# A two-branch encoder layer on one core: first loads in order of need, combinations in six pieces, the first mixer low parts on GpSimd, denominators in one operation, zero halves kept

## The chip, the cores and the metric

The kernel runs on one core of one Trainium2 chip, in one launch. The metric is the device time of an execution in microseconds (us). The engines are PE (TensorE, the matrix engine), ACT (ScalarE), DVE (VectorE), POOL (GpSimd) and SP (SyncE, which here only issues DMAs). All but SP compute; each works through its own list of instructions in the listed order and waits on semaphores for the others.

## The reference

One encoder layer is applied with shared weights to two inputs, `x_prompt` (1024 tokens, called A in the kernel) and `x_sample` (512 tokens, called B), model width 1024, everything in float32.

```python
def encoder_layer(x, ...):
    h = rms_norm(x, pre_w)
    cols = jnp.einsum('bsd,dc->bsc', h, w_in)
    m_qk, m_v, m_o, m_z, m_i, m_f, a_qkv, a_z, gate = jnp.split(cols, ...)
    y_m = mlstm_mixer(m_qk, m_v, m_o, m_i, m_f, ...) * jax.nn.silu(m_z)
    y_a = dilated_attention(a_qkv, rel_table) * jax.nn.silu(a_z)
    p_m = jnp.einsum('bsc,cd->bsd', y_m, w_pm)
    p_a = jnp.einsum('bsc,cd->bsd', y_a, w_pa)
    g = jax.nn.sigmoid(gate).reshape(b_, s_, N_BRANCHES, D_MODEL)
    merged = g[:, :, 0] * p_m + g[:, :, 1] * p_a
    out = jnp.einsum('bsd,de->bse', merged, w_out)
    return x + rms_norm(out, post_w)

def mlstm_scan(q, k, v, li, lf):          # per direction, 4 heads of 256, chunks of 128 tokens
    def step(carry, xs):
        ...
        num = jnp.einsum('nhts,nhsv->nhtv', sc, vc) + wa[..., None] * jnp.einsum('nhtk,nhkv->nhtv', qc, c_mat)
        den = jnp.sum(sc, axis=-1) + wa * jnp.einsum('nhtk,nhk->nht', qc, n_vec)
        h = num / jnp.maximum(jnp.abs(den), jnp.exp(-mt))[..., None]
        ...
```

The mLSTM runs forward and backward, and each head's sum of both is normalized. The attention has three groups of 8 heads of 64 with windows and dilations (128, 1), (512, 4), (2048, 16); each group adds a bias by relative distance (`rel_table`).

## The kernel before

**Arithmetic.** Every float32 product is made of three matmuls: each operand is split into a high part (rounded by a copy on ACT, `fp32r`) and a low part (the difference, made on DVE or POOL). `mm3` (L192 to L194) issues high × high, high × low, low × high into one PSUM bank. So ahead of any product stand an ACT copy and a subtraction.

**Stages.** The span begins with the values and gates of B (`short_values`, to about 145 us), then come the projections of A (to 1074), then four stages in which PE fills its waits with projections of B and of the mixers: the mLSTM of A (1095 to 1382), the attention of A, the mLSTM of B (`mlstm_short`), the attention of B with the closing projections.

**The start.** `short_values` (L356) works through eight blocks of 322 weight columns, `vw` tiles `va` and `vb` in turn, each in two halves `kh` (128x1288). A half is split into `vhi` (ACT, L375) and `vlo` (DVE, L376) and multiplied by the high and low parts `Hh`, `Hl` of B's transposed input, 96 matmuls of 128x322 a block in four banks `d`, one for each 128 tokens. The results are scaled by the inverse root of each token's mean square and copied out to `vz` (ACT L398, DVE L399) or `avz`. The loop loads block b+2 at its end, since its tile is then free.

Beside it run the roots: `scale(i)` (L1768) loads the rows of B, or one of two halves of A, ACT sums the squares (L255, one operation of 128x1024 for each 128 tokens), POOL makes the inverse root `xr` (L256, L257). `spread(i)` (L1774) turns four such columns into a row that is the same on all partitions: DVE puts each on a diagonal `dg` (L1777), PE multiplies them by ones, ACT copies the result to `R` (L313). With `R`, `combos` (L325) makes from A's transposed input `xq` the operands of A's projections, which are done with seven products of block matrices instead of eight: norms (L317), sums and differences, and their high and low parts (L321, L322).

**The order of the work.** From the start to 1074 us the order on each engine is set by a scheduler of the compiler, by priorities and by the order in the code; `tc.high_priority()` puts the block splits ahead, and `tc.issue_after(x)` keeps what is in its block behind instruction x on that engine's list. From the mixers on, the order of PE and SP is the order of the code. There loads go through a list: `queue` adds one, `tick` (once a round) issues `pace` of them, and `need` issues all up to the one asked for.

**The transition.** The last projections of A are two gates each (`gates(j, c)`); the first mixer unit of B is a dense projection with weights `wraw`, split into `wh` (ACT, L248) and `wl` (DVE, L249), on B's input `xs`, split by `short_input` (L640) into `H`.

**The mLSTM rounds.** A round is (head, chunk, direction), 64 in all for A. `front(k+1)` prepares the next round's operands, `core(k)` multiplies. Value tiles (`V0a` to `V1b`) have 258 columns: 256 values, a column of ones, which sums the denominator in the same product `num`, and a column of zeros. DVE makes the denominator in two operations and inverts it; in the second half of the chunks ACT squares and scales the sum `X` to `hn`, and three rounds later PE transposes it (L984):

```python
r = sb.tile([P, 4], F32, name="r", bufs=4)
nc.vector.tensor_scalar(r[:, 0:1], pn[:, 256:257], m["fl"], None, op0=OP.max)
nc.vector.scalar_tensor_tensor(r[:, 1:2], pn[:, 256:257], -1.0, r[:, 0:1], op0=OP.mult, op1=OP.max)
nc.vector.reciprocal(r[:, 2:3], r[:, 1:2])
```

**The attention units.** A unit u (0 to 11) is a pair of heads of one group. Units of the dilated groups whose sequence is 128 long are called narrow (8 of 12 for B, 4 of 12 for A). `att_load` puts a narrow unit's keys into `V0a`, `V0b`, `V1a`, `V1b` in such a way that each head's half is zero in the other head's place, with memsets on POOL (L1275), and queues the loads; `table` loads a unit's bias table as the unit begins.

Of the kernel before, what the change touches and what calls it, by code (L numbers as in the profile page):

```python
# [29 lines left out]
P = 128  # L30
# [145 lines left out]
class Net:  # L176
    def __init__(self, tc, a):
        self.tc, self.nc, self.a = tc, tc.nc, a
        self.clock = self.lag = 0
        self.pending, self.owner = [], {}  # L180
        self.defer, self.mixed, self.rows = False, set(), {}
        self.queued, self.pace = [], 1

# [59 lines left out]
    def split_w(self, raw, n):  # L243
# [3 lines left out]
        self.wsplit.append((hi, lo))  # L247
        self.splits = (nc.scalar.activation(hi[:, :n], raw[:, :n], AF.Copy),  # L248
                       nc.vector.tensor_sub(lo[:, :n], raw[:, :n], hi[:, :n].bitcast(F32)))  # L249
# [69 lines left out]
    def parts(self, hl, k, x):  # L319
        hi, lo = hl[0][:, k], hl[1][:, k]  # L320
        end = self.nc.scalar.activation(hi, x[:, k], AF.Copy)  # L321
        self.nc.vector.tensor_sub(lo, x[:, k], hi.bitcast(F32))  # L322
        return end

    def combos(self, H, xq, R):  # L325
# [12 lines left out]
        for k in range(4):  # L338
            self.norm(a1, 0, k, R[1])
            self.norm(b1, 1, k, R[1])  # L340
        for k in range(4):
# [16 lines left out]
    def short_values(self, T, H, load, vw, sb, ps, r, first, places):  # L358
# [5 lines left out]
        for b in range(8):  # L364
            raw = raws[b % 2]
            banks = [ps.tile([P, BLK], F32, name="d") for _ in range(4)]
            for kh in range(2):
                hi, lo = places.pop(0) if places else (vw.tile([P, N], F32R, name=x, bufs=2) for x in ("vhi", "vlo"))
                with self.tc.high_priority():
                    parts = 4 if b == 0 else 1  # L370
                    for i in range(parts):
# [4 lines left out]
                        nc.vector.tensor_sub(lo[:, c], raw[:, kh, c], hi[:, c].bitcast(F32))  # L376
                if b == 0:
                    load(kh, 4)
                wh, wl = (z.rearrange("p (k c) -> p k c", c=VW) for z in (hi, lo))
# [6 lines left out]
            if b < 6:  # L386
                raws[b % 2] = vw.tile([P, 2, N], F32, name=("va", "vb")[b % 2], bufs=1)
                fetch(b + 2)
            c0 = VW * b
            for t in range(4):  # L390
# [4 lines left out]
                if a0 < a1:  # L395
                    z, x = sb.tile([P, 2, VW], F32R, name="vz", bufs=3), p[:, a0 - c0:a1 - c0]
# [5 lines left out]
                if a0 < c0 + VW:  # L402
                    z, w = sb.tile([P, VW], F32, name="avz", bufs=3), c0 + VW - a0
# [236 lines left out]
    def short_input(self, xt):  # L640

        for q in range(2):
            for k in range(4):
                end = self.parts(self.hT[q], k, xt[q])
# [167 lines left out]
    def ml_load(self, T, h):  # L812
# [12 lines left out]
        for i, x in enumerate([both[0][:, :1032], both[0][:, 1032:]] if S == BLK else both):  # L825
            x = x.rearrange("p (n c) -> p n c", c=258)
            nc.gpsimd.memset(x[:, :, 256:257].bitcast(F32), 1.0 - i)
            nc.gpsimd.memset(x[:, :, 257:258].bitcast(F32), 0.0)
# [6 lines left out]
    def mlstm(self, T, fill, steps, first, banks, lead, after, beside=()):  # L835
# [10 lines left out]
        with ExitStack() as stack:  # L846
# [13 lines left out]
            fill.stage(steps, lead + len(rounds) + n // 4 + 3)  # L860
# [66 lines left out]
            def core(k):  # L927
# [37 lines left out]
                nc.vector.tensor_scalar(r[:, 0:1], pn[:, 256:257], m["fl"], None, op0=OP.max)  # L965
                nc.vector.scalar_tensor_tensor(r[:, 1:2], pn[:, 256:257], -1.0, r[:, 0:1], op0=OP.mult, op1=OP.max)
# [37 lines left out]
            for k, (h, i, d) in enumerate(rounds):  # L1004
# [16 lines left out]
                turns.pop(k - 3, lambda: None)()  # L1021
# [1033 lines left out]
```

## Time and profile before

| | us |
|---|---|
| median of 3 executions | 2307.6 (2307.18 to 2310.66) |
| the profiled execution | 2305.97 |
| its span, first to last instruction | 2304.2 |
| PE busy in the span | 2240.8 (97%) |
| DVE, ACT, POOL busy | 1483.5, 1104.3, 619.0 |

The mean granted clock of TensorE is 0.992. "Busy" counts an engine's instructions, register and DMA-issuing ones left out. A row of the timeline gives start, length, engine, line, operation, `output<-inputs`, shape and count, and in brackets the idle time of the engine just before it with what ended that. A row of the waits says for whom an engine waited, in all, how often, and the longest.

### The profile page before, as it was taken

The page shows a single profiled execution, that of the slowest core. Times are in us where ns is not written, and L with a number is a line of the kernel's source. Part 1 is how long each engine was busy: PE and PEld are TensorE (multiplying, and loading weights), DVE is VectorE, ACT ScalarE, POOL GpSimd, SP SyncE. Part 2 cuts the span into 40 slices and gives each one's busy share as a digit, 9 for nine tenths or more (in the row PEclk, how much of TensorE's full clock was granted, in tenths as well). Part 3 has the DMA queues.
Part 4 walks back from the last instruction along what each step waited for, and adds up shares of the span by engine and source line. Part 5 has one row for each costly group of instructions (what it writes and reads, how often), then busy time and mean ns, then how long its engine had stood idle before and what let it go on. Part 6 is the DMA issues. An engine that isn't in the chain of part 4 may idle for free. (4 is left out here: it accounts for less than half of the span.)

```text
span 2304.2 us, 35360 instructions
## 1 busy us (share of the span) xinstructions
PE 2240.8 (97%) x12210; PEld 1955.1 (85%) x12210; DVE 1483.5 (64%) x2890; ACT 1104.3 (48%) x2255; POOL 619.0 (27%) x824
## 2 busy tenths in 40 slices
PE   8999999999999999998999999999999999999998
PEld 7999998888887888887888889989888888878787
DVE  3857656767888765644788876675477744555563
ACT  5534223434444433333777766676644444544332
POOL 1000003333333222230567650001033221421321
PEclk8999999999999999999999999999999999999999
DMA  9446424555422222434766569988777787686673
GB/s 360 146 122 155 130 95 171 195 192 194 153 107 104 92 83 93 149 111 143 260 213 208 153 175 241 239 232 213 205 240 253 236 255 229 190 261 195 214 258 113
DMA packets 253627, 425.05 MB, mean 184 GB/s; under 512 B 26208, under 2 KB 150752, under 8 KB 252680
## 3 DMA queue, kind: packets, MB, share of 16 engines
q1 hardware_dynamic: 249848, 410.20, 57.4%
q10 hardware_dynamic: 3600, 12.59, 1.4%
q8 instruction: 97, 1.59, 0.3%
q14 instruction: 82, 0.67, 0.1%
HBM read 302.72 MB, written 128.37 MB: 187 GB/s over the span
## 5 line engine op out<-in xcount | busy, mean ns | idle before, releaser
L192 PE MATMUL dense<-H,wh 128*128 128x512 f32 x672 | 281.1, 418 | 3.8 <-ACT wh L248 3.8
L194 PE MATMUL dense<-H,wl 128*128 128x512 f32 x672 | 265.6, 395 | 1.9 <-DVE wl L249 1.9
L193 PE MATMUL dense<-H,wh 128*128 128x512 f32 x672 | 264.8, 394 | 0.0
L194 PE MATMUL d<-Hh,phla 128*128 128x512 f32 x608 | 236.9, 390 | 1.8 <-DVE phla L527 1.8
L193 PE MATMUL d<-Hl,phla 128*128 128x512 f32 x608 | 236.6, 389 | 0.0
L192 PE MATMUL d<-Hh,phla 128*128 128x512 f32 x608 | 236.5, 389 | 0.0
L192 PE MATMUL d<-vhi,Hh 128*128 128x322 f32 x704 | 222.6, 316 | 7.4 <-ACT vhi L375 7.4
L193 PE MATMUL d<-vlo,Hh 128*128 128x322 f32 x704 | 222.3, 316 | 6.1 <-DVE vlo L376 6.1
L194 PE MATMUL d<-vhi,Hl 128*128 128x322 f32 x704 | 222.1, 316 | 0.0
L249 DVE TENSOR_TENSOR wl<-wraw,wh 128x1024 fp32r<-128x1024 f32 x110 | 138.3, 1258 | 80.1 <-ACT wh L248 74.5
L1371 DVE CUSTOM_DVE_ANT_0 ls<-lg,bias 128x256 f32<-128x256 f32 (+1 forms) x288 | 93.7, 362 | 148.5 <-PE lg L1359 60.9
L545 POOL TENSOR_TENSOR psum_w<-pw_raw 128x512 f32<-128x512 f32 x38 | 56.6, 1489 | 465.3 <-DMA pw_raw<-w_in 424.9
L192 PE MATMUL d<-Hh,phlb 128*128 128x512 f32 x456 | 177.4, 389 | 0.0
L193 PE MATMUL d<-Hl,phlb 128*128 128x512 f32 x456 | 177.4, 389 | 0.0
L194 PE MATMUL d<-Hh,phlb 128*128 128x512 f32 x456 | 177.4, 389 | 0.0
L1375 ACT ACTIVATE ls<-ls,nm 128x256 f32<-128x256 f32 (+1 forms) x288 | 130.0, 453 | 93.4 <-DVE nm L1373 83.4
L194 PEld LDWEIGHTS dense<-H,wl 128*128 128x128 f32 x672 | 126.9, 189 | 31.7 <-DVE wl L249 2.6
L248 ACT ACTIVATE wh<-wraw 128x1024 fp32r<-128x1024 f32 x110 | 115.7, 1053 | 72.4 <-PE dense L193 33.4
L192 PEld LDWEIGHTS d<-vhi,Hh 128*128 128x128 f32 x704 | 135.3, 192 | 9.2 <-ACT vhi L375 8.1
L192 PEld LDWEIGHTS dense<-H,wh 128*128 128x128 f32 x672 | 127.5, 190 | 17.5 <-ACT wh L248 4.2
L193 PEld LDWEIGHTS d<-vlo,Hh 128*128 128x128 f32 x704 | 135.2, 192 | 7.4 <-DVE vlo L376 7.4
L193 PEld LDWEIGHTS dense<-H,wh 128*128 128x128 f32 x672 | 127.7, 190 | 13.4
(558 smaller groups left out, 5708.3 us busy)
## 6 DMA issues: line engine op xcount, KB each, us to landing
pw_raw<-w_in SPq DMA_DIRECT2D x76, 512.0 KB
wraw<-w_in SPq DMA_DIRECT2D x76, 512.0 KB
aqk_a<-pwk SPq DMA_DIRECT2D x48, 512.0 KB
aqk_b<-sw SPq DMA_DIRECT2D x48, 256.0 KB
wraw<-w_pm SPq DMA_DIRECT2D x24, 512.0 KB
wraw<-w_out SPq DMA_DIRECT2D x24, 512.0 KB
vb<-w_vp SPq DMA_DIRECT2D x16, 644.0 KB
va<-w_vp SPq DMA_DIRECT2D x14, 644.0 KB
```

The source lines that it names most:

```text
L192: nc.tensor.matmul(out, lh, rh, start=start, stop=False)
L193: nc.tensor.matmul(out, lh, rl, start=False, stop=False)
L194: nc.tensor.matmul(out, ll, rh, start=False, stop=stop)
L248: self.splits = (nc.scalar.activation(hi[:, :n], raw[:, :n], AF.Copy), nc.vector.tensor_sub(lo[:, :n], raw[:, :n], hi[:, :n].bitcast(F32)))
L249: nc.vector.tensor_sub(lo[:, :n], raw[:, :n], hi[:, :n].bitcast(F32)))
L545: self.nc.gpsimd.tensor_add(s[:, 0], ws[1][:, 0], ws[1][:, 1])
L1371: nc.vector.tensor_tensor_reduce(out=ls[:, hh], in0=ts["lg"][hh], in1=bt[:, hh], scale=1.0, scalar=NEG, op0=OP.add, op1=OP.max, accum_out= ...
L1375: nc.scalar.activation(ls[:, hh], ls[:, hh], AF.Exp, bias=nm[:, hh:hh + 1], accum_out=ot[:, 128 + hh:129 + hh])
```

## The change

It has eight parts.

1. The first loads are issued in another order (below), and the loads of block b+2 ahead of block b's matmuls, in `short_values`. `spread(1)` comes after block 1 and `spread(2)` after block 2, instead of both after block 2. Pools: `vz` 3 to 8 buffers, `avz` 3 to 2, `dg` 8 to 4.
2. `combos` is cut into six pieces instead of five, and each stands behind the low part of a block's second split (`N.low`) on its engine.
3. The first mixer unit's weight low part `wl` and the low parts of the first half of B's input go from DVE to POOL (`low_on`, `on`), and `short_input` stands behind the two weight splits.
4. The column of zeros of the value tiles becomes −1, so that `num` holds the denominator with both signs, and one operation takes the largest of three.
5. `hn` is transposed four rounds later instead of three, for A.
6. A narrow unit's key tile with its zero halves is kept for the next one but one (`narrow`), so only the first two do the memsets.
7. A narrow unit also queues the bias table of the next unit (`tables`).
8. Line numbers move by 2 to 26.

```diff
-    def parts(self, hl, k, x):
+    def parts(self, hl, k, x, on=None):
         hi, lo = hl[0][:, k], hl[1][:, k]
         end = self.nc.scalar.activation(hi, x[:, k], AF.Copy)
-        self.nc.vector.tensor_sub(lo, x[:, k], hi.bitcast(F32))
+        (on or self.nc.vector).tensor_sub(lo, x[:, k], hi.bitcast(F32))
...
         for k in range(4):
             self.norm(a1, 0, k, R[1])
             self.norm(b1, 1, k, R[1])
+        yield
         for k in range(4):
             sub(a0[:, k], a1[:, k], a0[:, k])
...
-                        nc.vector.tensor_sub(lo[:, c], raw[:, kh, c], hi[:, c].bitcast(F32))
-                if b == 0:
-                    load(kh, 4)
-                wh, wl = (z.rearrange("p (k c) -> p k c", c=VW) for z in (hi, lo))
+                        self.low = nc.vector.tensor_sub(lo[:, c], raw[:, kh, c], hi[:, c].bitcast(F32))
+                split.append([z.rearrange("p (k c) -> p k c", c=VW) for z in (hi, lo)])
+            if b == 0:
+                load(1, 4)
+            if b < 6:
+                raws[b % 2] = vw.tile([P, 2, N], F32, name=("va", "vb")[b % 2], bufs=1)
+                fetch(b + 2)
+            if b == 0:
+                load(1, 5)
+            for kh, (wh, wl) in enumerate(split):
                 for i in range(4):
...
-            if b < 6:
-                raws[b % 2] = vw.tile([P, 2, N], F32, name=("va", "vb")[b % 2], bufs=1)
-                fetch(b + 2)
...
-                end = self.parts(self.hT[q], k, xt[q])
+                end = self.parts(self.hT[q], k, xt[q], None if q else self.nc.gpsimd)
...
-            nc.gpsimd.memset(x[:, :, 256:257].bitcast(F32), 1.0 - i)
-            nc.gpsimd.memset(x[:, :, 257:258].bitcast(F32), 0.0)
+            if i:
+                nc.gpsimd.memset(x[:, :, 256:258].bitcast(F32), 0.0)
+            else:
+                for c in range(2):
+                    nc.gpsimd.memset(x[:, :, 256 + c:257 + c].bitcast(F32), 1.0 - 2 * c)
...
-            fill.stage(steps, lead + len(rounds) + n // 4 + 3)
+            fill.stage(steps, lead + len(rounds) + n // 4 + 4)
...
-                nc.vector.tensor_scalar(r[:, 0:1], pn[:, 256:257], m["fl"], None, op0=OP.max)
-                nc.vector.scalar_tensor_tensor(r[:, 1:2], pn[:, 256:257], -1.0, r[:, 0:1], op0=OP.mult, op1=OP.max)
+                nc.vector.tensor_scalar(r[:, 1:2], pn[:, 256:257], m["fl"], pn[:, 257:258], op0=OP.max, op1=OP.max)
...
-                turns.pop(k - 3, lambda: None)()
+                turns.pop(k - 4, lambda: None)()
...
+        kept = None if wide else self.narrow.get((S, u % 2))
...
+                    if kept is None:
+                        nc.gpsimd.memset(k[i][rows, :, 1 - side].bitcast(F32), 0.0)
...
             b0 = table(0)
+            if u < 11:
+                self.tables[u + 1] = bias()[:, :2 * P].rearrange("p (h w) -> p h w", h=2)
+                self.table_load(T, u + 1, 0, self.tables[u + 1])
...
-                    elif j:
-                        scale(0)
+                    elif k == 4:
                         for kh in range(2):
                             weights(1, kh)
-                        xq.extend([xp.tile([P, 4, BLK], F32, name=f"xq{2 * i + j}") for j in range(2)] for i in range(2))
-                        for i in range(2):
-                            scale(1 + i)
-                        for i in range(2):
-                            for j in range(2):
-                                nc.sync.dma_start(xq[i][j], a[x1 + "_t"][i, j])
+                        scale(0)
+                    else:
+                        scale(1)
+                        inputs(0)
+                        scale(2)
...
                 next(steps)
+                spread(1)
+                inputs(1)
                 next(steps)
-                for i in (1, 2):
-                    spread(i)
+                spread(2)
...
-                for b, _ in enumerate(steps):
+                with tc.issue_after(N.low.ins):
                     next(combos)
+                for b, _ in enumerate(steps):
+                    with tc.issue_after(N.low.ins):
+                        next(combos)
...
+            N.low_on.append(nc.gpsimd)
...
-            end = N.short_input(xt)
+            with tc.issue_after(N.splits[0].ins), tc.issue_after(N.splits[1].ins):
+                end = N.short_input(xt)
```

The order on SP at the start, before. `vb` and `va` of shape 128x1288 are the weight halves of blocks 1, 2 and 3, `Hh_…` and `Hl_…` loaded from `x_sample` and `x_prompt` are rows for the roots (they lie in buffers of later operands), and `xq` is A's transposed input.

```order
L1771 DMA Hh_102<-x_sample 128x1024 x2
L1771 DMA Hl_109<-x_sample 128x1024 x2
L1763 DMA vb<-w_vp 128x1288 x2
L1771 DMA Hh_101<-x_prompt 128x1024 x2
L1771 DMA Hl_108<-x_prompt 128x1024 x2
L1771 DMA Hh_99<-x_prompt 128x1024 x2
L1771 DMA Hl_106<-x_prompt 128x1024 x2
L1805 DMA xq_283<-x_prompt_t 128x2048
L1805 DMA xq_284<-x_prompt_t 128x2048
L1805 DMA xq_285<-x_prompt_t 128x2048
L1805 DMA xq_286<-x_prompt_t 128x2048
L362 DMA va<-w_vp 128x1288 x2
```

The same place after it:

```order
L1779 DMA vb<-w_vp 128x1288 x2
L1787 DMA Hh_102<-x_sample 128x1024 x2
L1787 DMA Hl_109<-x_sample 128x1024 x2
L1787 DMA Hh_101<-x_prompt 128x1024 x2
L1787 DMA Hl_108<-x_prompt 128x1024
L365 DMA va<-w_vp 128x1288 x2
L1787 DMA Hl_108<-x_prompt 128x1024
L1824 DMA xq_254<-x_prompt_t 128x2048
L1824 DMA xq_255<-x_prompt_t 128x2048
L1787 DMA Hh_99<-x_prompt 128x1024 x2
L1787 DMA Hl_106<-x_prompt 128x1024 x2
```

Block 1's weights moved ahead of all rows, block 2's ahead of one row tile of A's first half and all of the second; two `xq` loads and then the weights of block 3 follow behind these rows.

The order on ACT around blocks 2 and 3, before (`R_144`, `R_145` are the rows that `spread(1)` and `spread(2)` make, `xr` the columns of roots):

```order
L375 ACTIVATE vhi<-vb 128x1288
L398 ACTIVATE vz<-d,xr_131 128x322
L398 ACTIVATE vz<-d,xr_132 128x322
L398 ACTIVATE vz<-d,xr_133 128x322
L375 ACTIVATE vhi<-vb 128x1288
L398 ACTIVATE vz<-d,xr_134 128x322
L313 ACTIVATE R_144<-d 128x512
L313 ACTIVATE R_145<-d 128x512
L321 ACTIVATE Hh_98<-xq_283 128x512 x4
```

After it, from block 1's third copy to the first half of the combinations:

```order
L405 ACTIVATE vz<-d,xr_133 128x322
L257 ACTIVATE Hl_108,xr_138<-Hl_108 128x1024
L379 ACTIVATE vhi<-va 128x1288
L405 ACTIVATE vz<-d,xr_134 128x322
L315 ACTIVATE R_144<-d 128x512
L323 ACTIVATE Hh_98<-xq_254 128x512 x4
```

And a few rows on, at block 3's split:

```order
L257 ACTIVATE Hl_106,xr_142<-Hl_106 128x1024
L276 ACTIVATE cws<-cws 128x32
L277 ACTIVATE cws<-cws 128x32
L315 ACTIVATE R_145<-d 128x512
L379 ACTIVATE vhi<-vb 128x1288 x2
L405 ACTIVATE vz<-d,xr_131 128x322
```

A root of A's first half now stands among block 1's copies, with `R_144` right behind them, and `R_145` has moved ahead of both high parts of block 3.

The order on POOL at the transition, before (`V0a` to `V1b` are the value tiles, `sraw` a buffer of the mixers):

```order
L563 TENSOR_TENSOR psum_w<-pw_raw,psum_w 128x512 x2
L827 MEMSET V0a 128x8
L828 MEMSET V0a 128x8
L827 MEMSET V0b 128x8
L828 MEMSET V0b 128x8
L827 MEMSET V1a 128x8
L828 MEMSET V1a 128x8
L827 MEMSET V1b 128x8
L828 MEMSET V1b 128x8
L590 MEMSET sraw 128x1
```

After it:

```order
L570 TENSOR_TENSOR psum_w<-pw_raw,psum_w 128x512 x2
L838 MEMSET V0a 128x8 x2
L835 MEMSET V0b 128x8x2
L838 MEMSET V1a 128x8 x2
L835 MEMSET V1b 128x8x2
L251 TENSOR_TENSOR wl_8709<-wraw_8706,wh_8708 128x1024
L324 TENSOR_TENSOR H_8721<-xs_7664,H_8720 128x512 x4
L597 MEMSET sraw 128x1
```

The weight's low part and four low parts of the input came from DVE; they stand behind the memsets of the value tiles. On DVE remain the low parts of the second weight and of the second input half.

40 lines of the change are left out of this document (24 added, 16 removed).

## The prediction

> **What bounds the kernel now.** I read the page's first part, then busy time in stretches of the span (each row: from and to, length, busy us and instructions of PE, its weight loads, DVE, ACT and POOL, then the granted clock, the DMA share and GB/s), then what TensorE (PE) waits for (us in total, times, longest), and last the timeline at each place that the diff touches.
>
> ```profile
> PE 2240.8 (97%) x12210; PEld 1955.1 (85%) x12210; DVE 1483.5 (64%) x2890; ACT 1104.3 (48%) x2255; POOL 619.0 (27%) x824
> 145.00:691.00 546.00, 546.00 (x2860) 485.10 (x2860) 391.28 (x480) 206.92 (x243) 130.40 (x104) 1.00 0.46 152
> 1095.00:1382.00 287.00, 275.26 (x1724) 244.79 (x1724) 229.22 (x552) 208.16 (x517) 178.03 (x313) 0.99 0.64 202
> 20.00:90.00 70.00, 56.70 (x340) 55.21 (x339) 40.14 (x65) 35.77 (x64) 7.61 (x19) 0.88 0.76 267
> 90.00:130.00 40.00, 40.00 (x272) 40.00 (x271) 21.37 (x29) 17.87 (x28) 0.34 (x2) 1.00 0.44 150
> 48.00:58.00 10.00, 10.00 (x61) 10.00 (x61) 2.71 (x4) 2.25 (x6) 0.00 (x0) 0.88 1.02 322
> 1165.90:1176.00 10.10, 10.10 (x52) 8.96 (x53) 6.83 (x19) 7.42 (x21) 6.29 (x18) 0.83 0.48 145
> 2072.40:2082.00 9.60, 9.54 (x37) 7.83 (x38) 4.66 (x18) 5.12 (x17) 2.03 (x3) 0.71 1.01 279
> PE d L192 <- ACT vhi L375: 7.4, 2, 4.3
> PE d L193 <- DVE vlo L376: 6.1, 4, 4.1
> PE a L984 <- ACT hn L977: 6.3, 4, 2.2
> PE num L192 <- ACT X L969: 2.0, 3, 1.1
> PE num L192 <- DVE r L966: 1.8, 1, 1.8
> PE a L1183 <- ACT hn L1176: 5.5, 6, 1.3
> ```
>
> PE is busy for 2240.8 of 2304.2 us, so 63.4 us of idle time, and whatever a lowered clock costs, is all that a reordering can win. From 145 to 691 us PE has no idle time at all: what the start gains shifts the rest forward whole. The waits name where much of the 63.4 lies: value splits 13.5, mLSTM transposes 6.3, their counterpart of the short batch 5.5.
>
> The start loses more than its gaps. From 90 to 130 us, at full clock and without a gap, 272 matmuls pass in 40 us, 6.80 a microsecond. The 340 of the stretch from 20 to 90 would need 50.0 us and took 70: 20.0 us lost. Busy time of 56.70 leaves 13.3 us of gaps; the other 6.7 is the granted clock, 0.88 on average there, and low even in a row without a gap (48 to 58: 61 matmuls in 10 us instead of 68).
>
> **Part 1: first loads and block splits.** The three gaps and what they stand on:
>
> ```profile
> 23.45 0.64 PE L192 MATMUL d<-vhi,Hh 128*128 128x322 f32 x1 [3.11 <-ACT vhi L375]
> ...
> 46.01 0.64 PE L192 MATMUL d<-vhi,Hh 128*128 128x322 f32 x1 [4.32 <-ACT vhi L375]
> ...
> 83.75 0.42 PE L193 MATMUL d<-vlo,Hh 128*128 128x322 f32 x1 [4.08 <-DVE vlo L376]
> 44.68 1.28 ACT L375 ACTIVATE vhi<-va 128x1288 fp32r<-128x1288 f32 x1 [10.48 <-DMA va<-w_vp]
> 68.05 10.02 DVE L317 SCALAR_TENSOR_TENSOR xq<-xq,prew,R 128x512 f32<-128x512 f32 x15
> 77.98 4.30 DVE L322 TENSOR_TENSOR Hl<-xq,Hh 128x512 fp32r<-128x512 f32 x7
> 82.20 1.50 DVE L376 TENSOR_TENSOR vlo<-va,vhi 128x1288 fp32r<-128x1288 f32 x1
> ```
>
> Block 1 (gap at 23.45) splits its weights on ACT behind row sums whose rows were loaded first. Block 2's weights arrive at 44.68, last of the line. The new order puts 6.5 MB behind them (four 1 MB `xq` pieces, five 512 KB row tiles), 20 to 24 us at the 322 and 267 GB/s of the rows above, so they come between 20 and 25; block 1, which could start at 20.3 (23.45 − 3.11), ends near 35. At 82.20 the low part stands behind 14 us of combinations, queued on DVE without regard to it; in six pieces behind the splits it goes ahead of them. These gaps, their second halves and the clock behind them go: up to 20.0 us.
>
> Two waits come instead, both read from the order. First, PE now does `spread(1)` right after block 1, and its fourth diagonal needs a row sum that ACT makes among the value copies of block 1. Second, in block 3 ACT writes `R_145` (from `spread(2)`, after block 2 on PE) ahead of both high parts `vhi<-vb`. Prices:
>
> ```profile
> 26.68 1.06 ACT L255 ACTIVATE Hl<-Hl 128x1024 f32<-128x1024 f32 x1
> 30.75 0.55 POOL L257 TENSOR_TENSOR xr<-xr,mhalf 128x1 f32<-128x1 f32 x1
> 65.40 0.86 DVE L1777 TENSOR_SCALAR dg<-ident,xr 128x128 f32<-128x128 f32 x4
> 66.86 1.08 ACT L313 ACTIVATE R<-d 128x512 f32<-128x512 f32 x2
> ```
>
> Row sum 1.06, its POOL root 0.55, a diagonal 0.22: 1.8 us, of which the copies of block 1 hide little; with the steps between engines I take 2 us of idle PE. Block 3: R 0.54, high part 1.28, then the low part, 1.50: 3.3 us. Together 5.3. The gap of 1.85 us shown further down is followed by a granted clock of 0.83 over 10.10 us (the row from 1165.90), 1.7 us lost; with one such loss the new waits cost 7.0, and the start gives 20.0 − 7.0 = 13. Ends: both waits hidden, 20; each half as long again and two clock losses, 11.3, so 8.7. The combinations cost nothing while DVE has room: a block is 96 matmuls at 6.80, 14.1 us, a piece of 12 operations at 0.67 (10.02 by 15) 8.0, two low parts 3.0. If that cover is gone, PE waits for what a piece overruns. **−13.**
>
> **Part 2: low parts of the first mixer projection on GpSimd.**
>
> ```profile
> 1077.70 0.66 PE L192 MATMUL dense<-H,wh 128*128 128x512 f32 x1 [3.77 <-ACT wh L248]
> ...
> 1080.66 0.79 PE L194 MATMUL dense<-H,wl 128*128 128x512 f32 x1 [1.88 <-DVE wl L249]
> 1074.58 4.90 DVE L322 TENSOR_TENSOR H<-xs,H 128x512 fp32r<-128x512 f32 x8
> 1079.39 2.35 DVE L249 TENSOR_TENSOR wl<-wraw,wh 128x1024 fp32r<-128x1024 f32 x2
> 1074.00 0.11 POOL L827 MEMSET V0a<- 128x8 f32 x1 [20.64 <-PE d L194]
> 522.12 4.90 DVE L631 SCALAR_TENSOR_TENSOR pwk<-c,pwk 128x1024 fp32r<-128x1024 f32 x2 [1.69 <-ACT pwk L630]
> 522.94 2.32 POOL L545 TENSOR_TENSOR psum_w<-pw_raw 128x512 f32<-128x512 f32 x1 [5.56 <-DMA pw_raw<-w_in]
> L563 POOL TENSOR_TENSOR psum_w<-pw_raw,psum_w x38: 1287/1302/1742, 347.2 to 1052.1; 128x512 f32<-128x512 f32 x38
> ```
>
> Here PE waits 3.77 for ACT's high parts, then 1.88 for DVE, which makes eight 128x512 low parts (0.61 each) before the weight's. Now ACT has the high parts done before PE's last pair ends (the order puts them ahead of the last copies of `gates(7)`), so the first wait goes. But `wl` and four low parts stand on POOL behind the memset that waits for PE until 1074.00: at 1.30 for 128x512, 2.6 + 4 × 1.30 = 7.8 us, to about 1082.1; the second matmul runs at about 1078.2, and one k-step per 1.30 after it. Before, the fourth k-step ended at about 1084.5: three steps of three matmuls, 0.43 each at the low clock there, after 1080.66. So −2.4. The other end is contention: POOL took 2.32 instead of 1.30 beside DVE's two-input operation at 522, and DVE owes 1.2 + 4 × 0.61 = 3.7 us of its own; if all of that excludes POOL, the fourth step is at 1085.8, +1.3. Neither row is nearer, so I take **−1**. [...]
>
> **Part 3: mLSTM rounds.** Dropping one of two denominator operations shortens DVE by 64 × 0.156, 10 us, and some 5 in the short batch; PE gains only where it waits for `r`. Transposes one round later (`k-4`) let PE find `hn` ready:
>
> ```profile
> 1165.90 0.36 PE L192 MATMUL num<-V0a,sch 128*128 128x258 f32 x1 [1.85 <-DVE r L966]
> L966 DVE SCALAR_TENSOR_TENSOR r<-num,r x64: 139/156/161, 1103.2 to 1364.9; 128x1 f32<-128x1 f32 x64
> ```
>
> A round is 287/64 = 4.5 us, longer than the longest wait on `hn` (2.2), so all 6.3 can go. Late next is `num`: 2.0 us on `X`, 1.85 on `r`, with DVE busy 80% (229.22 of 287). I let 1.3 come back: **−5** (ends: −10 with `r`'s wait and its clock loss of 1.7 gone too, −1 if the waits move to `num`). In the short batch the shorter chain takes 0.15 off each of six waits: **−1**.
>
> [...] At 1165.90, 1.85 us of idle time ran into the granted clock of 0.83. [...]
>
> **Part 4: zero halves and bias tables.**
>
> ```profile
> 2072.46 0.55 PE L192 MATMUL lg<-V1a,Q 128*128 128x256 f32 x1 [3.10 <-POOL V0a L1275]
> 2042.75 1.56 POOL L1275 MEMSET V1a<- 64x512 f32 x3
> ```
>
> Memsets leave POOL, which is busy 27%. The one PE wait put down to them comes 30 us after that tile's memsets (2042.75), so a load, I think, ended it: 0, with −5.9 as the other end (3.10, and 0.29 × 9.6 = 2.8 us of clock in the row from 2072.40). Tables one unit earlier: no wait of PE names them, 0.
>
> **Sum.** 2305.97 − 13 − 1 − 5 − 1 = 2286.0 for the profiled execution; the median shown lies 1.6 above it. I forecast 2286 and leave the 1.6 to the range.
>
> **Rivals.** (a) The gain shrinks: start −8.7, mLSTM −1, POOL +1.3, short batch −1: 2297. For it: each new wait is on PE with nothing between, and DVE is at 80%. Against: the waits removed are larger. (b) All of it goes: start −20, mLSTM −10, POOL −2.4, short batch −1, 2072 −5.9: 2267. For it: block 3's split could come early; against it: `R_145` ahead of the high parts does not depend on a load. (c) The loads by need do nothing, since the line is full (share 1.02 from 48 to 58): block 3's weights, now last, are as late as block 2's were, and only the gap at 83.75 (4.08 and 1.7 of clock) is won: with the other terms 2293. Against it: a block of 14.1 us more lies ahead of them. (d) Slower: the table of the next narrow unit, queued on SP ahead of loads of the present one, delays its keys; each such unit repeats the case at 2072.46, 3.10 + 2.8 = 5.9 us. Four units (23.6) use up the forecast's 20 us; from the fifth on it is slower: five give 2315, eight 2333. For it: DMA share 1.01 there; against it: the tables have no more bytes than before, and most units show no such wait. (e) The gains of (a) meet two such units, 2309: within 0.2%.
>
> **How the numbers follow.** Forecast 0.50 (own range 2279 to 2292), (a) and (c) 0.24 together, (b) 0.14, (e) 0.06, (d) 0.06. A change below 0.2% (4.6 us) can't be told from none. Faster 0.88, same 0.06, slower 0.06. The range runs from 2271, towards (b), to 2300, past (a).
>
> **What would show it.** Right: no wait on `vhi` near 23 and 46, none on `vlo` at 83, new ones of 2 to 3 us near 35 and 52; the stretch from 20 to 90 holds some 430 matmuls; the projection's second matmul comes at POOL's pace; no waits of L984's transposes on `hn`; the wait at 2072 still there. Wrong: gaps near 35 and 52 of over 4 us with a clock near 0.5, a DVE piece that overruns each block, new waits on `num`, or waits on loads of keys in most narrow units.

## The result and the profile after

The changed kernel takes 2287.78 us (median of 4, 2285.19 to 2289.43) against 2307.97 (median of 4, 2307.18 to 2310.66): ratio 0.9909, 95% interval 0.9892 to 0.9927. That is 20.2 us less, where 2286 was forecast. The profiled execution took 2288.94, its span is 2287.1.

In the page of the profile PE's busy time has hardly changed (2240.8 before), since no matmul was added or removed:

```profile
span 2287.1 us, 35174 instructions
...
PE 2238.4 (98%) x12210; PEld 1951.7 (85%) x12210; DVE 1472.8 (64%) x2789; ACT 1101.6 (48%) x2255; POOL 612.3 (27%) x789
```

The waits of PE over the span (us in total, times, longest) say which ones went and which came:

```profile
PE dense L194 <- POOL H L324: 4.7, 1, 4.7
PE pt L1398 <- ACT ls L1391: 4.3, 5, 1.1
PE dense L193 <- DVE sw L1697: 4.2, 4, 1.6
PE num L193 <- ACT X L978: 2.3, 3, 1.1
PE lg L193 <- issue: 2.1, 1, 2.1
PE lg L193 <- DVE ot L1387: 2.1, 1, 2.1
PE kv L193 <- ACT hn L983: 2.0, 1, 2.0
PE d L193 <- ACT vhi L379: 1.9, 1, 1.9
PE num L193 <- DVE r L976: 1.6, 1, 1.6
PE a L1191 <- ACT hn L1184: 1.6, 2, 1.0
PE d L194 <- DVE vlo L380: 1.5, 2, 1.1
...
PE a L993 <- ACT hn L986: 0.7, 1, 0.7
```

The splits fell from 13.5 to 3.4, the transposes of A's mLSTM from 6.3 to 0.7, those of the short batch from 5.5 to 1.6. New at the top is GpSimd's low part, 4.7. The stretches of the start, with the columns of the prediction's rows:

```profile
20.00:90.00 70.00, 66.63 (x436) 66.02 (x435) 40.58 (x65) 41.40 (x75) 9.95 (x24) 0.98 0.85 301
48.00:58.00 10.00, 7.03 (x41) 6.61 (x40) 5.61 (x9) 4.30 (x6) 0.00 (x0) 0.89 1.08 278
```

From 20 to 90 us 436 matmuls pass instead of 340, where "some 430" were expected. Nearly all that is left of the loss stands in one place, block 3, in the last row.

A stage can be measured in two traces by the first or last matmul of one kind at its border. The last value matmul (`d<-vhi,Hl`) starts at 347.3 before and at 332.8 after:

```profile
L194 PE MATMUL d<-vhi,Hl x704: 303/312/473, 6.3 to 347.3; 128*128 128x322 f32 x176
```

```profile
L195 PE MATMUL d<-vhi,Hl x704: 303/312/473, 6.3 to 332.8; 128*128 128x322 f32 x176
```

Read in the same way from the groups `a<-ident,K`, `a<-ident,hn` and `a<-Q` of each trace, the time of each stage in us is as follows (the attention of B runs from the short mLSTM's last transpose to the end of the span):

| | before | after | difference |
|---|---|---|---|
| start to the last value matmul | 347.3 | 332.8 | −14.5 |
| from there to A's first `K` transpose | 744.9 | 744.2 | −0.7 |
| mLSTM of A, to its last `hn` transpose | 278.3 | 274.6 | −3.7 |
| attention of A, to the short batch's first product | 305.5 | 305.0 | −0.5 |
| short mLSTM, to its last `hn` transpose | 182.4 | 177.8 | −4.6 |
| attention of B and closing projections | 445.8 | 452.7 | +6.9 |

The first five rows sum to −24.0; the last gives 6.9 back, in this execution.

The second row joins two things. Its −0.7 lies wholly in the projections, up to the last product `d<-Hh,phlb` of the gates (1073.5 before, 1058.3 after, so 726.2 and 725.5 us); from there to the first `K` transpose, the transition itself, both traces have 18.7 us.

### The profile page after: what moved, and what is told of

Its sections match the earlier page's. It is cut to its first block, busy times and chain, and to the rows that moved or that the text cites. A ratio compares the mean times of both kernels' runs of the same rounds, so it can differ in the third digit from the quotient of the medians.

```text
span 2287.1 us, 35174 instructions
## 1 busy us (share of the span) xinstructions
PE 2238.4 (98%) x12210; PEld 1951.7 (85%) x12210; DVE 1472.8 (64%) x2789; ACT 1101.6 (48%) x2255; POOL 612.3 (27%) x789
## 5 line engine op out<-in xcount | busy, mean ns | idle before, releaser
L193 PE MATMUL d<-Hh,phlb 128*128 128x512 f32 x456 | 177.4, 389 | 0.0
L194 PE MATMUL d<-Hl,phlb 128*128 128x512 f32 x456 | 177.4, 389 | 0.0
L195 PE MATMUL d<-Hh,phlb 128*128 128x512 f32 x456 | 177.4, 389 | 0.0
L193 PEld LDWEIGHTS dense<-H,wh 128*128 128x128 f32 x672 | 127.7, 190 | 13.6
L195 PEld LDWEIGHTS d<-Hh,phla 128*128 128x128 f32 x608 | 114.1, 188 | 26.0 <-DVE phla L534 2.4
```

The lines of the kernel that those rows point to most:

```text
L193: nc.tensor.matmul(out, lh, rh, start=start, stop=False)
L194: nc.tensor.matmul(out, lh, rl, start=False, stop=False)
L195: nc.tensor.matmul(out, ll, rh, start=False, stop=stop)
```

## The experiments

All twelve kernels were timed in several rounds against the kernel before. They ran in three groups, each on one chip, with medians of the kernel before of 2305.06, 2305.13 and 2305.71; so kernels of one group compare best, and the stages of the traces compare across all.

**1. The start alone.** All parts but the first two are undone: the low parts go back to DVE, the denominators to two operations, the transposes to `k - 3`, memsets and tables to every unit.

> The changed kernel with everything undone but the start: first loads in order of need, spreads after blocks 1 and 2, combinations in six pieces behind the splits. Theory (the stages add up): in the two traces the last value matmul comes 14.5 us earlier (332.5 against 347.0), nothing behind the start is changed, so the whole time falls by 14 to 15 us, to about 2293.5. Rival (given back later): the attention of B took about 7 us longer in the changed kernel's trace although none of its matmuls changed; if that is the price of an earlier or differently phased start, this kernel shows it too and gains only 7 to 8, about 2300.

2293.08 (8 runs, 2287.83 to 2302.02), ratio 0.9948, interval 0.993 to 0.9965: 12 less, 8 to 16 by the interval. In its trace the start ends at 331.4, and the attention of B takes 445.5, as before (445.8). The gain of the start is passed on, and an earlier start does not lengthen the end. The stage sum stands; the rival's 7 to 8 lie just below the interval, and nothing in the trace supports it. (That the start gains 15.9 in this trace, and not 14.5, is the clock; see the last section.)

**2. Old loads, six pieces kept.**

```diff
-                        for kh in range(2):
-                            weights(1, kh)
                         scale(0)
+                        for kh in range(2):
+                            weights(1, kh)
...
                         scale(1)
-                        inputs(0)
                         scale(2)
+                        inputs(0)
+                        inputs(1)
...
-                spread(1)
-                inputs(1)
                 next(steps)
+                spread(1)
                 spread(2)
```

(and `fetch(b + 2)` at the block's end, the old buffer counts)

> The changed kernel with the old order of the first loads and the old place of the spreads (and the old buffer counts), but the combinations still in six pieces behind the splits. Theory: the loads by need carried two gaps (3.1 and 4.3 us with their second halves, 0.9 each) and two clock losses of 3.4, less the 3.0 us of new waits and one clock loss of 1.7 that they brought; the pieces only the gap at 83.75 and its clock, 5.8. So this kernel is about 9 us slower than the changed one, 2297, with the waits near 23 and 46 back and none near 83. Rival (the DMA line was full, so the order of loads does nothing): within 2 us of the changed kernel, 2288.

2295.97 (8 runs, 2288.98 to 2297.73), ratio 0.9956, interval 0.994 to 0.9973. Its start ends at 342.3, 9.5 later than with the new loads, and the two gaps are back in PE's timeline, with their second halves, while the one at 83 is not:

```profile
23.21 0.41 PE L193 MATMUL d<-vhi,Hh 128*128 128x322 f32 x1 [2.84 <-ACT vhi L379]
24.75 0.42 PE L194 MATMUL d<-vlo,Hh 128*128 128x322 f32 x1 [1.12 <-DVE vlo L380]
46.00 0.64 PE L193 MATMUL d<-vhi,Hh 128*128 128x322 f32 x1 [5.22 <-ACT vhi L379]
47.53 0.64 PE L194 MATMUL d<-vlo,Hh 128*128 128x322 f32 x1 [0.90 <-DVE vlo L380]
```

Of the 14.5 us at the start the order of the loads, with the place of the spreads and the buffer counts that were undone with it, carries 9.5, the pieces 5.0. That a full DMA line makes the order indifferent is refuted: in the changed kernel the line was as full (a share of 1.08 from 48 to 58 us, 1.02 before), and what was needed first came first: block 2's first high part begins at 30.82 us, against 44.68 before.

**3. The denominator in two operations again.**

```diff
-                nc.vector.tensor_scalar(r[:, 1:2], pn[:, 256:257], m["fl"], pn[:, 257:258], op0=OP.max, op1=OP.max)
+                nc.vector.tensor_scalar(r[:, 0:1], pn[:, 256:257], m["fl"], None, op0=OP.max)
+                nc.vector.scalar_tensor_tensor(r[:, 1:2], pn[:, 256:257], -1.0, r[:, 0:1], op0=OP.mult, op1=OP.max)
```

(and the same in the short batch)

> The changed kernel with the denominator made again in two DVE operations (the column of minus ones stays in the value tiles but is not read). Theory: the short batch's mLSTM took 4.6 us less in the changed kernel's trace, and this is the only part that touches its rounds, so the waits of the transposes on hn come back (5.5 us instead of 1.6) and the time rises by 4 to 5, to about 2292; the mLSTM of A loses under 1. Rival (my first reckoning, 0.15 us for each of six waits): it rises by 1 at most, and the short batch gained by another cause.

2296.26 (9 runs, 2291.92 to 2303.29), ratio 0.9962, interval 0.9945 to 0.9979. The short mLSTM is back at 182.3 us with all its waits on `hn`, as expected. Not expected: the mLSTM of A takes 283.6, 9 more than in the changed kernel's first trace, with waits of `num` on `r` and `X`:

```profile
PE a L1193 <- ACT hn L1186: 5.6, 6, 1.3
PE num L193 <- ACT X L979: 5.1, 3, 1.9
...
PE num L193 <- DVE r L977: 3.3, 1, 3.3
...
PE num L193 <- DVE X L982: 3.0, 2, 2.8
```

**4. The first mixer low parts back on DVE** (`low_on` empty, `short_input` without `gpsimd` and without its `issue_after`).

> The changed kernel with the first mixer low parts back on DVE and the input split no longer behind the weight splits (the transition as it was before). Theory: the two traces' stretches from the last projection pair to the first mLSTM transpose differ by 0.7 us, so this costs 0 to 1.5 us, with PE's two waits of 3.8 and 1.9 us back. Rival (GpSimd and DVE exclude each other, so moving work to GpSimd costs more than it saves): this kernel is faster than the changed one by 2 to 4 us.

2284.03 (5 runs, 2278.37 to 2288.42), ratio 0.9907, interval 0.9885 to 0.9929: no difference from the changed kernel that can be told (0.9909 and, below, 0.9919). The stretch to A's first transpose takes 745.5 against 744.2, with the waits of 3.8 and 1.7 back. The part is worth about a microsecond in the trace and nothing that the times show. The median is even 2.5 us below that of experiment 5, the sign that the rival had, but the trace doesn't put it at the transition: what is shorter there is the attention of B (442.5 against 446.2), which the part doesn't touch. From the last gate product to the first `K` transpose this trace has 19.4 us, experiment 1, also without the part, 19.6 and the kernel before 18.7; the eight traces with the part (the changed kernel's and experiments 2, 3, 5, 6, 7, 9 and 10) have 18.2 to 18.7.

**5. The changed kernel again.**

> The changed kernel itself once more, as the measure for the kernels beside it. Its first trace has the attention of B, from the last transpose of the short mLSTM to the end, at 452.7 us; the kernels so far, with and without the parts that touch this stage, have 442.5 to 445.8. If the 7 us are only this one execution (three spells of half clock lie in it), this trace shows about 445 and a span near 2280; if they belong to the kernel, 452 again.

2286.53 (4 runs, 2284.16 to 2288.31), ratio 0.9919, interval 0.9904 to 0.9934. The span is 2282.4 and the attention of B takes 446.2. The first trace's 452.7 was mostly that execution: in two stretches of this stage it had more idle time (3.9 and 8.1 us, here 3.6 and 3.5) and, in the first, a lower clock. The first trace, then this one:

```profile
1861.00:1907.80 46.80, 42.91 (x228) 36.02 (x227) 20.01 (x49) 21.38 (x55) 14.23 (x12) 0.93 0.96 268
1907.80:2055.00 147.20, 139.10 (x732) 117.44 (x731) 71.97 (x191) 66.75 (x184) 35.88 (x39) 0.99 0.76 213
```

```profile
1862.80:1908.00 45.20, 41.65 (x229) 35.13 (x228) 20.80 (x49) 21.03 (x55) 14.12 (x12) 0.96 0.93 272
1908.00:2050.00 142.00, 138.47 (x733) 117.40 (x732) 72.30 (x193) 67.37 (x185) 36.14 (x39) 0.99 0.77 222
```

**6. Three rounds again, one operation** (`turns.pop(k - 3, ...)` and `+ 3` in `fill.stage`).

> The changed kernel with the transposes of the mLSTM of A three rounds later again instead of four; the denominators stay in one operation. Theory (each part does its own work): the four waits on hn, 6.3 us, come back and 2 to 3 us of the waits on num go, so the mLSTM of A takes 277 to 278 us instead of 274.6 and the time rises by 3. Rival (the shorter denominator does the work, the fourth round none): hn comes early enough anyway, the stage stays at 274 to 275 and the time within 1 us. The kernel with two operations and four rounds had 283.6 in this stage, 5 more than with two operations and three rounds, which speaks for the rival.

2283.18 (4 runs, 2282.28 to 2284.80), ratio 0.9904, interval 0.9887 to 0.992. The mLSTM of A takes 274.2 us: the waits on `hn` are back (6.1 in seven), others went, and nothing is lost. The rival holds: a fourth round gains nothing (over all traces it costs about 2 us, see the table under 9 and 10).

**7. Memsets and tables at every unit again.**

```diff
-        if not wide:
-            self.narrow[S, u % 2] = kk
...
-            if u < 11:
-                self.tables[u + 1] = bias()[:, :2 * P].rearrange("p (h w) -> p h w", h=2)
-                self.table_load(T, u + 1, 0, self.tables[u + 1])
```

> The changed kernel with the memsets of the zero halves made for every narrow unit again and the bias tables loaded as each unit begins. Theory: no wait of PE stands on either, so both attention stages keep their length and the time stays within 2 us. Rival: they are what made the attention of B longer in the changed kernel's trace, then this one is 5 to 7 us faster; or, the other way, the wait of 2.8 to 3.1 us at the ninth narrow unit and its clock loss come back, 4 to 6 us slower.

2283.46 (4 runs, 2281.68 to 2285.01), ratio 0.9906, interval 0.9891 to 0.9921, the attention of B 444.3. Within what the executions differ by, neither part does anything. The wait at the narrow unit that the prediction left standing (2072.46 before) is 2.8 us here and 2.1 in the changed kernel, at the same product `lg<-V1a,Q`, so it was not the memsets'. In experiment 5, the changed kernel's second trace, no wait stands at that product. Here, then in the changed kernel:

```profile
2050.72 0.36 PE L193 MATMUL lg<-V1a,Q 128*128 128x256 f32 x1 [2.81 <-POOL K L1586]
```

```profile
2055.31 0.36 PE L193 MATMUL lg<-V1a,Q 128*128 128x256 f32 x1 [2.10 <-issue]
```

**8. The two waits that the change brought, taken away.**

```diff
-                spread(2)
                 for m in (T1, T3, T2):
...
                     with tc.issue_after(N.low.ins):
                         next(combos)
+                    if b == 0:
+                        spread(2)
...
-            if i:
-                nc.gpsimd.memset(x[:, :, 256:258].bitcast(F32), 0.0)
-            else:
...
+            with self.tc.issue_after(self.pool_end.ins):
+                if i:
+                    nc.gpsimd.memset(x[:, :, 256:258].bitcast(F32), 0.0)
+                else:
```

(`pool_end` is GpSimd's last low part)

> The changed kernel with two orders changed: the memsets of the value tiles stand behind the low parts on GpSimd, so that these need not wait for PE's last projection pair; and the second spread comes one block later, so that ACT makes the high parts of block 3 ahead of the second row. Theory: the wait of 4.7 us at the transition goes with a clock loss of 3.4, and the waits of 1.9 and 1.1 us at block 3 with one of 1.7: 10 to 11 us faster than the changed kernel. Rival: DVE's own low parts come next at the transition (they still wait for the last pair: 1.2 + 0.7 us behind it), and half of the 8 us there comes back: 6 to 7 faster.

2277.90 (4 runs, 2277.29 to 2278.10), ratio 0.9882, interval 0.9867 to 0.9896: 8.6 less than the changed kernel beside it. The start ends at 328.5, 4.4 earlier than there, as worked out. At the transition GpSimd is now done 3.6 us ahead of PE's last pair, and that wait is gone. Another takes its place, the loads of A's `K`, which SP issues as DVE finishes the last pair (1055.25 + 0.69, `Q` at 1055.96):

```profile
1044.21 2.41 POOL L251 TENSOR_TENSOR wl<-wraw,wh 128x1024 fp32r<-128x1024 f32 x1 [9.58 <-ACT wh L250]
1046.57 5.05 POOL L324 TENSOR_TENSOR H<-xs,H 128x512 fp32r<-128x512 f32 x4
...
1055.25 0.69 DVE L589 TENSOR_TENSOR c<-pu,d 128x512 f32<-128x512 f32 x1 [2.03 <-PE d L195]
...
1056.99 2.49 DVE L324 TENSOR_TENSOR H<-xs,H 128x512 fp32r<-128x512 f32 x4
...
1055.96 0.80 SPq L230 DMA_DIRECT2D Q<-qk_a  x2
1056.86 0.86 SPq L230 DMA_DIRECT2D K<-qk_a  x2
...
1064.66 0.46 PE L883 MATMUL a<-Q,K 128*128 128x128 f32 x2 [1.98 <-DMA K<-qk_a]
1067.14 3.33 PE L883 MATMUL a<-Q,K 128*128 128x128 f32 x14 [2.02 <-DMA K<-qk_a]
```

So the stretch from the start to the first transpose of A gains 0.9 (743.0 against 743.9 us) instead of the 8 of the theory or the 4 that the rival leaves. Neither had named this wait. The 8.6 in the medians lies between the theory's 10 to 11 and the rival's 6 to 7; the two places account for 5.3 of it, the spans differ by 6.3 (2276.1 and 2282.4), and the rest is no more than executions differ by.

**9 and 10. The square of denominators and rounds filled up.**

> The changed kernel with two denominator operations and three rounds, the fourth corner of the square of denominators (one or two operations) and rounds (four or three). Measured so far for the mLSTM of A: one operation and four rounds 274.6 and 277.0, one and three 274.2, two and four 283.6. Theory (the short chain does the work and a fourth round only helps or harms through DVE's queue): like the kernel before, 276 to 278 in this stage, with the waits on hn back, the short batch at 182 instead of 177.5; in all 6 to 8 us slower than the changed kernel, about 2293. Rival (the fourth round by itself costs 5 with two operations by chance of one execution): then 283 here too, about 2299.

> Two operations and four rounds once more, beside the corner above. Theory: 283 again in the mLSTM of A, since num waits on DVE's r and X there, and 5 us slower than the kernel with two operations and three rounds. Rival (one slow execution): 277, and the same time as that kernel.

2287.66 (6 runs, 2281.09 to 2296.33), ratio 0.9924, interval 0.9903 to 0.9945, and 2298.53 (11 runs, 2293.99 to 2302.18), ratio 0.9964, interval 0.9952 to 0.9976. The mLSTM of A in all traces of this case, in us:

| | three rounds | four rounds |
|---|---|---|
| two operations | 278.3 (before), 275.8 (experiment 1), 275.0 (9) | 283.6 (3), 282.6 (10) |
| one operation | 274.2 (6), 275.1 (11), 273.9 (12) | 274.6 (changed kernel), 277.0 (5), 274.9 (2), 276.8 (4), 276.7 (7), 277.6 (8) |

The short mLSTM: 182.7 and 182.6 with two operations, 177.4 to 177.8 with one. By stages both theories hold: four rounds with two operations cost 7 to 8 us in A's, as before, and the short batch is at 182. By time the tenth kernel is 10.9 slower than the ninth where 5 were expected, and the ninth 5 faster than expected. That the tenth is slower is clear, since the intervals do not meet; how much is less so, with the ninth's executions 15 us apart. One operation alone gives A about 2 (with three rounds, means of 276.4 and 274.4) and the short batch 5; a fourth round takes A's 2 back (mean 276.3). The attention of A behind it is 2 to 4 us longer in the three kernels with two operations here (307.6 in experiment 3, 308.7 and 308.9) than in all others (304.3 to 305.6), the kernel before and experiment 1, which also have two, among them; the cause of that is open. In the tenth kernel the longest waits of that stage stand on the denominator's column and on `X`:

```profile
1150.69 0.40 PE L193 MATMUL num<-V0a,sch 128*128 128x258 f32 x1 [3.48 <-DVE r L977]
...
1332.98 0.55 PE L193 MATMUL num<-V1a,sch 128*128 128x258 f32 x1 [2.83 <-DVE X L982]
```

From the first operation of the denominator to the end of the reciprocal a round of A takes 1.35 us on average there, against 1.21 in the ninth kernel. Why the order with four rounds is so much more exposed was not tried further.

**11 and 12. The two waits off with three rounds, and with memsets and tables at every unit as well.**

> The kernel with the two waits off (memsets behind the low parts on GpSimd, second spread one block later) and three rounds instead of four. Three rounds were 3.3 us faster than four in the medians (2283.2 against 2286.5), of which 2.8 stands in the mLSTM of A (274.2 against 277.0). Theory (that difference is real and adds): 2275. Rival (the two are the same within what one kernel's executions differ by): 2278, as with four rounds.

> The same with the zero halves set for every narrow unit and the bias tables loaded as each unit begins. That undoing was 3.1 us faster in the medians (2283.5 against 2286.5) though no wait in the traces stands on either. Theory (they cost and gain nothing): the same as the kernel beside it, within 2 us. Rival: 3 faster again, then the tables or the kept halves do cost something in the attention of B.

2275.49 (4 runs, 2272.24 to 2275.88), ratio 0.9865, interval 0.9846 to 0.9884, and 2279.77 (6 runs, 2269.39 to 2280.87), ratio 0.9879, interval 0.9858 to 0.9901. The first is the fastest version here: 30 us below the kernel before of its group, and faster than the changed kernel (the intervals 0.9846 to 0.9884 and 0.9892 to 0.9927 do not meet). Three rounds against four stays inside the overlap of the intervals of the eighth and eleventh; memsets and tables at every unit, 3 faster in experiment 7, are 4 slower here, so they do nothing that the times show.

These two traces also say what the eighth kernel's order at the transition is worth. From the last gate product to A's first `K` transpose experiment 5 has 18.2 us, the eighth kernel 16.7, the eleventh 14.9 and the twelfth 13.6, the last three with the same order there and each with the waits on `K` (4.0, 2.7 and 3.0 us). The granted clock tells them apart: in that stretch it is at half for 6.8 us in experiment 5, for 6.5 in the eighth, for 3.2 in the eleventh, and not at all in the twelfth. So the order gave 1.5 to 4.6 us, and the eighth kernel's trace shows the low end.

## Why the prediction held, step by step

**The start (forecast −13, measured −14.5).** The mechanism held as written. Of the two new waits the second is exactly where it was put and nearly as priced, 1.85 and 1.12 us, together 3.0 against 3.3, with one spell of half clock (0.89 in the row from 48):

```profile
35.78 0.49 PE L314 MATMUL d<-dg,ones 128*128 128x128 f32 x2 [0.40 <-DVE dg L1793]
...
53.37 0.41 PE L193 MATMUL d<-vhi,Hh 128*128 128x322 f32 x1 [1.85 <-ACT vhi L379]
54.91 0.42 PE L194 MATMUL d<-vlo,Hh 128*128 128x322 f32 x1 [1.12 <-DVE vlo L380]
```

The first was over-sized: 0.40 instead of 2. PE finishes the four banks one after the other, and ACT's row sum begins when the third is copied (33.35), so the fourth bank's matmuls and six of the spread's eight hid most of it. That is about the 1.5 us of difference. The measured 14.5 lies by chance near 14.7, the 20.0 less 5.3 that no loss of clock would have left: the loss came, and experiment 1, without it, has 15.9.

**The transition (−1, measured 0.0 in the first pair of traces; against experiment 4: −0.7 to −1.2).** The −0.7 of the table is close to the forecast by luck, since it lies ahead of the transition. Over all traces the part is worth 0 to 1.4 us (18.2 to 18.7 us with it, 18.7 to 19.6 without), so the middle between the ends was right in size, but the rows say that the pessimistic one described what GpSimd and DVE did. The two engines at that place:

```profile
1062.42 6.81 DVE L324 TENSOR_TENSOR H<-xs,H 128x512 fp32r<-128x512 f32 x4
...
1061.38 7.30 POOL L324 TENSOR_TENSOR H<-xs,H 128x512 fp32r<-128x512 f32 x4
```

Apart, these take 2.49 and 5.05 us (experiment 8), 7.54 in all. Here 7.85 us passed from the start of GpSimd's to the end of DVE's: they gained nothing by running side by side, as if the two engines took turns. So the step "one k-step per 1.30" failed: the second matmul of each of the first four k-steps stands at 1063.68, 1065.36, 1067.05 and 1068.74, one per 1.69 us. That cost little, because PE at half clock needs 1.28 us for a k-step anyway (three matmuls of 0.43), before as after.

**The mLSTM of A (−5, measured −3.7 and, in experiment 5, −1.3).** The step "transposes one round later let PE find `hn` ready, so all 6.3 can go" failed as a statement on time: the waits on `hn` did go (0.7), but the stage is as short with three rounds. Others came in their place (`kv`, 2.0, in the rows of the waits after), those of `num` on `X` and `r` stayed (3.9 against 3.8), and PE's idle time in the stage fell only from 11.6 to 9.1 us, in experiment 5 to 10.0. Nor does the −3.7 repeat: the kernel before's 278.3 is the longest of the three traces with its denominators and rounds (mean 276.4), the changed kernel's 274.6 the shortest of six (mean 276.3). So the gain of this stage is not shown; the prediction's low end, −1 if the waits move, comes nearest to what the traces show.

**The short batch (−1, measured −4.6).** The step that failed is "the shorter chain takes 0.15 off each of six waits". The price was that of one operation, taken from its own row; but the two operations were not next to each other on DVE. At one place of that stage, a long one, the first (L1165) begins at 1720.79 and the reciprocal (L1167) at 1722.98, 2.2 us later, though the two operations before it take only 0.35; in the changed kernel the reciprocal begins 0.3 us after the one operation. Before, then after:

```profile
1720.79 0.21 DVE L1165 TENSOR_SCALAR r<-num,col 128x1 f32<-128x1 f32 x1
1720.92 0.88 DVE L1126 TENSOR_TENSOR rm<-col,rw 128x384 f32<-128x384 f32 x2
...
1721.90 0.14 DVE L1166 SCALAR_TENSOR_TENSOR r<-num,r 128x1 f32<-128x1 f32 x1
...
1722.98 0.15 DVE L1167 RECIPROCAL r<-r 128x1 f32<-128x1 f32 x1
```

```profile
1701.65 0.27 DVE L1174 TENSOR_SCALAR r<-num,col 128x1 f32<-128x1 f32 x1
1701.85 0.15 DVE L1509 TENSOR_TENSOR cw<-cw,V0b 128x8 f32<-128x8 f32 x1
1701.96 0.16 DVE L1175 RECIPROCAL r<-r 128x1 f32<-128x1 f32 x1
```

That the denominator is the cause is shown by the third, ninth and tenth kernels, whose short batch is back at 182; that it is this spacing is read from the rows. Over the 32 rounds of the stage, the time from the first operation to the end of the reciprocal is 1.23 us on average before and 0.92 after. DVE's own time was over-sized instead: the merged operation takes 0.27, not 0.21, so each saves 0.09 rather than 0.15.

**Zero halves and tables (0, measured 0).** As written; experiments 7 and 12 lie on either side of none. The rival (d), a delayed key load in each narrow unit, did not happen: PE's waits on loads of keys in the attention of B are 1.5 us in all after, 1.6 before.

**The sum.** The stages up to the attention of B give −24.0 in the first trace and, with the second trace of the changed kernel, −22.2 (1858.4 to 1836.2). The forecast of −20 held in the time because its misses have both signs: start 1.5 and short batch 3.6 too small, the mLSTM of A 1 to 4 too large; and the last stage differs by several us from one execution to the next (442.5 to 452.7 over all traces). That the number came within 2 us is in part luck: the mechanism held at the start, which is most of it, while the short batch gained by another step than the one that was priced.

## What to carry to other kernels

When the first loads fill the line, issue them in the order in which the bound engine needs them, and then look at what each in-order engine has queued in front of the newly first work: that, not the transfer, was the next wait here (`R_145` on ACT ahead of block 3's high parts, 1.85 us). An operation taken out of a dependent chain on a shared in-order engine was worth its own time plus what the scheduler had put between it and the next link (0.31 us a round in the short batch, 0.09 of it its own), so read the neighbouring rows, not only its duration. Where a wait is removed, name what arrives next at the same matmul: here GpSimd's low part (4.7 us) had covered the load of `K` (4.0 us in experiment 8). And measure a stage in several traces before a part is credited with it: the 3.7 us of A's mLSTM in one pair were gone in the mean of all.

## What the runs showed of the hardware

Read one by one, short gaps meet the half clock irregularly: idle times of 1.79 and 2.19 us in the ninth kernel's trace were followed by a granted clock of 1.00, where the kernel before had 0.83 after 1.85. The start shows it best. The changed kernel's first trace and that of experiment 1 have the same two gaps at block 3, 1.85 and 1.12 us, and the clock halves in the first alone. The changed kernel, then experiment 1 (PE's busy us are the third number, the granted clock the third from the end):

```profile
49.05:52.46 3.41, 2.47 (x19) 2.28 (x17) 0.96 (x4) 0.90 (x2) 0.00 (x0) 1.00 1.07 355
52.46:55.87 3.41, 1.38 (x7) 1.15 (x8) 2.52 (x2) 2.87 (x4) 0.00 (x0) 1.00 1.12 193
55.87:59.29 3.42, 3.42 (x15) 3.42 (x14) 3.42 (x6) 1.42 (x3) 0.00 (x0) 0.50 1.03 285
```

```profile
49.96:53.38 3.42, 1.65 (x14) 1.45 (x12) 0.96 (x4) 1.74 (x3) 0.00 (x0) 1.00 1.09 298
53.38:56.79 3.41, 2.21 (x13) 1.99 (x14) 3.35 (x3) 2.74 (x6) 0.00 (x0) 1.00 1.09 215
56.79:60.20 3.41, 3.41 (x25) 3.41 (x24) 3.41 (x7) 2.77 (x5) 0.00 (x0) 1.00 1.02 370
```

In each of the fourteen traces of this case all changes of the granted clock lie whole multiples of 3.41 us apart, on a grid that stands at another place of the span each time; the stretches above are cut on it. In the first trace 2.03 us of the idle time fall into one stretch, and the next runs at half clock; in the second the same gaps are shared out between two stretches, 1.77 and 1.20, and the clock stays. Counted over all 9240 such stretches at full clock, half clock followed each of the 45 in which PE was idle for 1.88 us or more, 21 of the 82 with 1.34 to 1.87, and none of the others. So in these traces the half clock goes with the idle time within a stretch of the grid, not with the length of one gap, and the same code at one place lost 1.7 us (half of 3.41) in one trace and nothing in the other. The middle may be blurred, since the profile models the ends of matmuls.
